# A gated-DeltaNet mixer written out in the order of its source, in a two-layer decoder trunk

## The chip, the core and the metric

The kernel runs on one core of a Trainium2 chip. A core has several engines, each with its own stream of instructions: TensorE (PE) for matrix products, VectorE (DVE), ScalarE (ACT), GpSimd (POOL) and SyncE (SP), which here mostly issues DMAs. They meet through semaphores. The metric is the device time of one execution in microseconds (us), the median of several.

## The reference

A trunk of two layers over 256 tokens of width 1024, in float32. Each layer is: half a SwiGLU FFN, a token mixer, cross-attention into 256 memory tokens, half a SwiGLU FFN, each behind an RMSNorm, with a residual sum. In layer 0 the mixer is dilated sliding-window attention beside a gated linear recurrence. In layer 1 it is the chunked gated DeltaNet:

```python
def deltanet_mixer(h, w_in, conv_w, a_log, dt_bias, o_norm, w_out):
    qkv, z, a, b = jnp.split(h @ w_in, [3 * W, 4 * W, 4 * W + DN_HEADS], axis=-1)
    qkv = jax.nn.silu(causal_dwconv(qkv, conv_w))          # 4 taps along the tokens
    q, k, v = jnp.split(qkv, 3, axis=-1)                   # 8 heads of 128
    q, k = l2norm(q.reshape(shp)), l2norm(k.reshape(shp))
    beta = jax.nn.sigmoid(b)
    g = -jnp.exp(a_log) * jax.nn.softplus(a + dt_bias)
    o = gated_delta_rule_chunked(q, k, v.reshape(shp), g, beta)  # chunks of 64: a triangular inverse,
    o = rmsnorm(o, o_norm) * jax.nn.silu(z.reshape(shp))         # then a state carried over the chunks
    return o.reshape(B, S, W) @ w_out
```

## The kernel before

Products are made to float32's accuracy from two parts: every weight and every moving operand is split into a high part and the rest. A weight arrives as `raw` by a DMA on SP; ScalarE copies it to its high part (L158), VectorE subtracts to get the low part (L159). One such conversion covers a half of a *unit*: 4 of the 8 blocks of 128 along the inner dimension, 256 columns wide. A unit is 256 columns of a weight against all tokens, in four *quarters*, each of 4 blocks for 128 columns (half of the unit's columns). In a quarter PE alternates a matmul of 512 columns (L200, high part) with one of 256 (L204, low part). After each quarter `tick` runs: after the first and the second it converts the two halves of the next unit's weight, and it runs pieces that fall due by the count of ticks (`self.after(n, fn)`).

The second mixer (in `mixer1`) has 16 units, in pairs of heads: `k0` is the keys of heads 0 and 1, likewise `q`, `v` and the gate `z`; `K2` and `K3` are units of the memory's keys and values for the cross-attention. `DN_ORDER` gives their order, with the groups of pairs `01` and `23` at the points where their recurrence is run:

```python
DN_ORDER = ('k0 k1 q0 q1 k2 v0 k3 v1 z0', '01|v3 z1 v2 q2', 'q3', '23|z2 z3 K2 K3')
```

Ahead of `k0` stand the normalisation (eight pieces: VectorE's product L409 into `xn`, ScalarE's high part L310, VectorE's rest L311 into `x2`) and a unit `ab` 128 columns wide for the gates a and b, with a softplus of 16 columns (L731 to L737). Each quarter-pair of a `k`, `q` or `v` unit is followed by `conv`: ScalarE copies the psum (L270), VectorE adds the second half of it (L271) into `xn`, ScalarE multiplies with the last tap (L1071), VectorE adds three more taps in place (L1074). When both halves are there, `silu` follows, as a tanh on ScalarE and a product on VectorE (L1080, L1081) for the units in `TWICE` (k0 k1 q0 q1), as ScalarE's own Silu (L1083) for the others. Then come squares (L1097) and sums over heads with a power of −1/2 on POOL (L341), the decays of a pair (`e`: a mask brought by SP, rows added by a DMA on POOL at L1119, exponentials at L1125, products at L1169), and a triangular inverse in steps (L1233 and L1235). The recurrence of a group (PE L1268 and L1274) runs in rounds; between rounds `fill(bg, n)` puts in n quarters of units from a background list. `DN_FILL` holds these numbers for the two groups. After it, `gated` (squares on ScalarE, POOL's power, VectorE L1332 and L1339) and `gated_T` (PE L1348, VectorE L1350 into `a`), and the output product.

The kernel is written in Tile, whose scheduler may move instructions within their engines: in before everything but the set-up has its order from it, and the source order counts only as a wish. In the first mixer, too, the heads' scores, weights and values are interleaved with quarters from a background list.

Of the kernel before, what the change touches and what calls it, by code (L numbers as in the profile page):

```python
# [9 lines left out]
F32 = mybir.dt.float32  # L10
# [3 lines left out]
AF = mybir.ActivationFunctionType  # L14
# [7 lines left out]
KD = 8  # L22
# [3 lines left out]
NEG = -1e30  # L26

DN_ORDER = ('k0 k1 q0 q1 k2 v0 k3 v1 z0', '01|v3 z1 v2 q2', 'q3', '23|z2 z3 K2 K3')
DN_FILL = ((1, 1, 1, 1, 1, 1, 1, 1, 1, 2, 2, 1), (1, 1, 1, 1, 1, 1, 1, 1, 1, 1, 1, 0, 5, 0))
YB = 5  # L30
EB, QB, VB = (4, 3, 3)
TWICE = 'k0 k1 q0 q1'.split()
# [35 lines left out]
class Net:  # L68
    def __init__(self, tc, t):
        self.tc, self.nc, self.t = tc, tc.nc, t  # L70
        self.raws, self.halves = {}, {}
        self.plan = list(self.make_plan())
        self.queue = [(i, k) for i, u in enumerate(self.plan) for k in range(0, u[4], 4)]

        self.queue[1], self.queue[2] = self.queue[2], self.queue[1]
        self.n_load = self.n_half = self.n_take = 0
        self.later = deque()
        self.banks, self.n_bank = "w", 0
        self.now, self.due = 0, []

# [62 lines left out]
    def split_half(self, step=4):  # L145

        nc = self.nc
        i, k = self.queue[self.n_half]
        name, l, _, _, nk, cols = self.plan[i]
        self.load_to(self.n_half + 1)  # L150
        n = min(4, nk - k)
        wt = self.p_wt.tile([P, 4, 2, 256], F32R, name="wt")
        raw = self.raws.pop(self.n_half)
        self.n_half += 1
        for u in range(0, n, step):
            us = slice(u, min(n, u + step))
            a, b, r = wt[:, us, 0, :cols], wt[:, us, 1, :cols], raw[:, us, :cols]
            nc.scalar.activation(a, r, AF.Copy)  # L158
            nc.vector.tensor_sub(b, r, a.bitcast(F32))  # L159
        self.halves.setdefault(i, []).append(wt)  # L160

    def w(self, name, c0):
# [10 lines left out]
    def tick(self):  # L173

        if self.n_half < len(self.queue) and self.queue[self.n_half][0] <= self.n_take:
            self.split_half()
        if self.later:
            self.later.popleft()()
        self.now += 1
        while self.due and self.due[0][0] <= self.now:  # L180
            self.due.pop(0)[2]()

    def after(self, n, fn):

# [5 lines left out]
    def mm3(self, out, wts, cols, mov, ks, k0=0, start=0, stop=KD):  # L190

        nc = self.nc
        for k in ks:
            i = k - k0
            w = wts[i // 4][:, i % 4]

            def high():
                nc.tensor.matmul(out.rearrange("p a s -> p (a s)"), w[:, 0, cols], mov[:, k].rearrange("p a s -> p (a s)"),  # L200
                                 start=k == start, stop=k == stop - 1)

            def low():
                nc.tensor.matmul(out[:, 0], w[:, 1, cols], mov[:, k, 0], start=False, stop=False)  # L204

            for part in (low, high) if k == stop - 1 else (high, low):
                part()

    def mm3t(self, out, mov, tok, wts, ks):

        nc = self.nc
        for k in ks:
            w = wts[k // 4][:, k % 4]

            def high():
                nc.tensor.matmul(out.rearrange("p a s -> p (a s)"), mov[:, k, 0, tok], w.rearrange("p a s -> p (a s)"),  # L216
                                 start=k == 0, stop=k == KD - 1)

            def low():
                nc.tensor.matmul(out[:, 0], mov[:, k, 1, tok], w[:, 0], start=False, stop=False)  # L220

            for part in (low, high) if k == KD - 1 else (high, low):
                part()
# [15 lines left out]
    def parts(self, out, a, b, first=True, last=True):  # L239

        for i, (u, w) in enumerate(((0, 0), (0, 1), (1, 0))):
            self.nc.tensor.matmul(out, a[u], b[w], start=first and i == 0, stop=last and i == 2)  # L242

    def unit_split(self, name, c0, mov, dst, tokens=False):

# [149 lines left out]
    def residual(self, k, ps, coef, gbase, parts=2):  # L395
        for i in range(parts):
            self.nc.vector.scalar_tensor_tensor(self.xT[:, k], ps[:, i], coef, self.xT[:, k],
                                                op0=OP.mult, op1=OP.add)
        if gbase == "sq":
            self.norm_sq(k)  # L400
        elif gbase is not None:
            self.norm_piece(k, gbase)
# [408 lines left out]
    def mixer0(self, mid, kT_mem, mem_mov, gnext):  # L811
        nc, tc, t = self.nc, self.tc, self.t
        mov = self.x2
        self.banks = "w"
        a2 = mid.tile([P, KD, 2, S], F32R, name="a2")
        with tc.tile_pool(name="m0", bufs=1, reuse_waits="tile") as mp:
# [9 lines left out]
            bg = deque()  # L826
# [33 lines left out]
            def scores(h):  # L860
                pr, par = divmod(h, 2)
                sc = self.bank("f")
                scf = sc.rearrange("p a b -> p (a b)")
                nc.tensor.matmul(scf[:, :P], qz[:, pr, par, :P], kT[:, pr, :P], start=True, stop=True)
                nc.tensor.matmul(scf[:, P:3 * P], qz[:, pr, par, P:], kT[:, pr], start=True, stop=True)
                pe = mp.tile([P, 2, S], F32, name="pe", bufs=3)
                mx = mp.tile([P, 2], F32, name="mx_a", bufs=3)
                nm = mp.tile([P, 2], F32, name="nm_a", bufs=3)
                den = mp.tile([P, 2], F32, name="den_a", bufs=3)
                rng = ((0, P), (P, 3 * P))  # L870
                for i, (u, w) in enumerate(rng):
                    nc.vector.tensor_tensor_reduce(pe[:, i, :w - u], scf[:, u:w], nmf[:, u:w], 1.0, NEG,
                                                   op0=OP.add, op1=OP.max, accum_out=mx[:, i:i + 1])
                nc.vector.tensor_scalar(nm, mx, -1.0, None, op0=OP.mult)
                for i, (u, w) in enumerate(rng):
                    nc.scalar.activation(pe[:, i, :w - u], pe[:, i, :w - u], AF.Exp, bias=nm[:, i:i + 1],
                                         accum_out=den[:, i:i + 1])
                return pe, den

            def weights(pe, den):  # L880
                ps = self.probs_T(pe, den, (P, 2 * P), mp)
                pT = mp.tile([P, 2, S], F32, name="pT_a", bufs=2)
                nc.scalar.activation(pT[:, 0], ps[:, 0], AF.Copy)
                nc.scalar.activation(pT[:, 1, P:], ps[:, 1, P:], AF.Copy)
                return pT

            def values(h, pT, po):

                pr, par = divmod(h, 2)
                o = po[:, par]  # L890
                vh = v[:, :, pr * P:pr * P + P]
                nc.tensor.matmul(o[:, :P], vh[:, 0], pT[:, 0, :P], start=True, stop=True)
                nc.tensor.matmul(o[:, P:], vh[:, 0], pT[:, 0, P:], start=True, stop=False)
                nc.tensor.matmul(o[:, P:], vh[:, 1], pT[:, 1, P:], start=False, stop=True)
                hs = slice(par * 64, par * 64 + 64)
                self.split(a2[hs, pr], o[hs])
# [52 lines left out]
            sc, pts, po = {}, {}, None  # L949
            for h in range(10):  # L950
                if h < 8:
                    sc[h] = scores(h)
                if 1 <= h < 9:
                    pts[h - 1] = weights(*sc.pop(h - 1))
                if h >= 2:
                    i = h - 2
                    if i % 2 == 0:
                        po = self.bank("s")
                    values(i, pts.pop(i), po)
                self.fill(bg, 2)  # L960
            self.fill(bg)
            self.flush()
            self.project_out("ab_w_out", a2, gnext)
# [37 lines left out]
    def mixer1(self, mid, kT_mem, mem_mov, gnext):  # L1001
        nc, tc, t = self.nc, self.tc, self.t
        mov = self.x2
        self.banks = "w"
        a2 = mid.tile([P, KD, 2, S], F32R, name="a2")
        with tc.tile_pool(name="m1", bufs=1, reuse_waits="tile") as mp:
            tok = lambda c: slice(c * P, c * P + P)

            nea, dtb = self.gate
# [376 lines left out]
            for i, part in enumerate(DN_ORDER):  # L1386
# [4 lines left out]
                group, bg = part.split("|")  # L1391
                gens = [back(int(p)) for p in group]
                bg = deque(unit(step) for step in bg.split())
                parts = list(DN_FILL[i // 2])
                if i == 1:
# [15 lines left out]
                    gated_T(int(p))  # L1411
                self.fill(bg)
            self.project_out("dn_w_out", a2, gnext)

    def finish(self):
        nc, tc = self.nc, self.tc
# [60 lines left out]
```

## Time and profile before

| | |
|---|---|
| median of 3 runs | 1252.77 us (1252.73 to 1253.04) |
| the profiled execution | 1251.99 us, of which the trace spans 1250.2 |
| PE busy | 1236.0 us, 99% |
| VectorE busy | 929.0 us, 74% |
| ScalarE busy | 752.0 us, 60% |
| conversions L159 / L158 | 484.9 us x409 / 418.6 us x409 |
| second mixer, first product to output product | 782.7 to 953.6 us |

An engine's busy time is the sum of its instructions' spans; a row of a timeline gives start, length, engine, line, operation, output and inputs, and in brackets how long the engine was idle before it and what it waited for. The line numbers are those of the kernel before.

### The profile page before, as it was taken

What the parts mean: (1) busy time and instruction counts of PE and PEld (TensorE: products, weight loads), DVE (VectorE), ACT (ScalarE), POOL (GpSimd) and SP (SyncE); (2) the same over time, 40 slices, a digit from 0 to 9 for tenths busy, and PEclk for the clock granted to TensorE, in tenths of its full rate; (3) what the DMA queues carried; (4) which work ended last, traced back from release to release, by engine and by line L of the source; (5) the groups of instructions that cost most, each with busy time, mean ns of one, the idle gap of its engine ahead of it and who ended that gap; (6) DMA issues with size and microseconds to landing.
All of it is one profiled execution on the core that took longest, in us unless ns stands there. A gap on an engine that the chain in (4) does not pass through costs nothing.

```text
span 1250.2 us, 20300 instructions
## 1 busy us (share of the span) xinstructions
PE 1236.0 (99%) x7702; PEld 1104.9 (88%) x7702; DVE 929.0 (74%) x1590; ACT 752.0 (60%) x1281; POOL 80.5 (6%) x96
## 2 busy tenths in 40 slices
PE   9999999999999999999999999999999999999997
PEld 8888889888998888888888888888898998888887
DVE  6987957788668778766877756989757668777753
ACT  7766545886555665545656544776757465666543
POOL 1000020000101000011000001020001101000000
PEclk9999999999999999999999999999999999999999
DMA  8766676544544566557666566667534535666561
GB/s 272 215 206 197 185 255 185 178 125 152 185 135 154 185 198 184 183 185 231 187 187 195 181 192 204 183 153 193 142 99 135 181 124 169 185 186 194 177 194 60
DMA packets 231019, 222.92 MB, mean 178 GB/s; under 512 B 14969, under 2 KB 228617, under 8 KB 230793
## 3 DMA queue, kind: packets, MB, share of 16 engines
q1 hardware_dynamic: 229448, 217.94, 56.9%
q0 software_dynamic: 1152, 3.15, 1.0%
q8 instruction: 60, 0.98, 0.3%
q10 hardware_dynamic: 320, 0.53, 0.1%
q14 instruction: 39, 0.31, 0.1%
HBM read 215.03 MB, written 5.51 MB: 176 GB/s over the span
## 4 chain that ended last, share of the span: by engine, by line
PE 90%; DVE 5%; ACT 2%; DMA 1%; issue 1%; POOL 1%; ACTq 0%; DVEq 0%; POOLq 0%
PE psw L200 21%; PE pss L200 16%; PE psw L204 11%; PE psf L200 11%; PE pss L204 8%; PE psf L204 5%; PE psw L242 5%; PE psf L242 4%; PE pss L242 3%; PE psw L216 2%; DVE wt L159 1%; PE psw L220 1%; ACT wt L158 1%; PE pss L1268 1%; PE psf L1274 1%
## 5 line engine op out<-in xcount | busy, mean ns | idle before, releaser
L159 DVE TENSOR_TENSOR wt<-raw,wt 128x1024 fp32r<-128x1024 f32 (+1 forms) x409 | 484.9, 1191 | 202.8 <-ACT wt L158 199.6
L158 ACT ACTIVATE wt<-raw 128x1024 fp32r<-128x1024 f32 (+1 forms) x409 | 418.6, 1031 | 172.1 <-PE psw L204 59.4
L200 PE MATMUL psw<-x,wt 128*128 128x512 f32 x864 | 310.6, 396 | 2.1 <-DVE xn L271 1.8
L204 PE MATMUL psw<-x,wt 128*128 128x256 f32 x864 | 224.9, 281 | 0.5 <-DVE wt L159 0.5
L200 PE MATMUL pss<-x,wt 128*128 128x512 f32 x520 | 187.4, 393 | 0.0
L200 PEld LDWEIGHTS psw<-x,wt 128*128 128x128 f32 x864 | 160.6, 188 | 30.1 <-issue 2.1
L204 PEld LDWEIGHTS psw<-x,wt 128*128 128x128 f32 x864 | 162.4, 188 | 9.4 <-DVE wt L159 1.0
L204 PE MATMUL pss<-x,wt 128*128 128x256 f32 x520 | 134.9, 280 | 0.0
L200 PE MATMUL psf<-x,wt 128*128 128x512 f32 x352 | 127.2, 394 | 0.0
L200 PEld LDWEIGHTS pss<-x,wt 128*128 128x128 f32 x520 | 97.7, 188 | 16.9 <-ACT bc L377 0.4
L204 PEld LDWEIGHTS pss<-x,wt 128*128 128x128 f32 x520 | 97.7, 188 | 5.4
L200 PE MATMUL psw<-h,wt 128*128 128x512 f32 x264 | 94.9, 396 | 0.0
L204 PE MATMUL psf<-x,wt 128*128 128x256 f32 x352 | 91.3, 280 | 0.0
L200 PE MATMUL pss<-h,wt 128*128 128x512 f32 x242 | 87.0, 396 | 0.0
L336 POOL TENSOR_TENSOR acc<-acc,sq 128x256 f32<-128x256 f32 x49 | 43.7, 891 | 658.3 <-ACT sq L334 557.3
L200 PEld LDWEIGHTS psf<-x,wt 128*128 128x128 f32 x352 | 66.1, 188 | 11.2
L204 PE MATMUL psw<-h,wt 128*128 128x256 f32 x264 | 72.0, 280 | 0.0
L204 PEld LDWEIGHTS psf<-x,wt 128*128 128x128 f32 x352 | 66.2, 188 | 3.5
L204 PE MATMUL pss<-h,wt 128*128 128x256 f32 x242 | 66.0, 280 | 0.0
L200 PEld LDWEIGHTS psw<-h,wt 128*128 128x128 f32 x264 | 49.6, 188 | 10.8
L200 PE MATMUL psf<-h,wt 128*128 128x512 f32 x154 | 55.4, 397 | 0.0
L200 PEld LDWEIGHTS pss<-h,wt 128*128 128x128 f32 x242 | 45.5, 188 | 9.8
(377 smaller groups left out, 2109.2 us busy)
## 6 DMA issues: line engine op xcount, KB each, us to landing
raw<-in_ffn_w_in_dram SPq DMA_DIRECT2D x175, 512.0 KB, 3.6
raw<-in_ffn_w_out_dram SPq DMA_DIRECT2D x80, 512.0 KB, 3.6
raw<-in_xa_wkv_dram SPq DMA_DIRECT2D x32, 512.0 KB, 3.5
raw<-in_dn_w_in_dram SPq DMA_DIRECT2D x32, 512.0 KB, 4.6
raw<-in_ab_w_in_dram SPq DMA_DIRECT2D x20, 512.0 KB, 3.6
raw<-in_xa_wq_dram SPq DMA_DIRECT2D x16, 512.0 KB, 3.5
raw<-in_xa_wo_dram SPq DMA_DIRECT2D x16, 512.0 KB, 3.4
raw<-in_ffn_w_out_dram SPq DMA_DIRECT2D x16, 256.0 KB, 2.9
```

Of the source, the lines that this page charges most:

```text
L158: nc.scalar.activation(a, r, AF.Copy)
L159: nc.vector.tensor_sub(b, r, a.bitcast(F32))
L200: nc.tensor.matmul(out.rearrange("p a s -> p (a s)"), w[:, 0, cols], mov[:, k].rearrange("p a s -> p (a s)"), start=k == start, stop=k == ...
L204: nc.tensor.matmul(out[:, 0], w[:, 1, cols], mov[:, k, 0], start=False, stop=False)
L216: nc.tensor.matmul(out.rearrange("p a s -> p (a s)"), mov[:, k, 0, tok], w.rearrange("p a s -> p (a s)"), start=k == 0, stop=k == KD - 1)
L220: nc.tensor.matmul(out[:, 0], mov[:, k, 1, tok], w[:, 0], start=False, stop=False)
L242: self.nc.tensor.matmul(out, a[u], b[w], start=first and i == 0, stop=last and i == 2)
L336: (eng or nc.gpsimd).tensor_add(self.acc, self.acc, sq)
L1268: nc.tensor.matmul(py[:, i], na[:, i], tu[:, 0, i], start=True, stop=True)
L1274: nc.tensor.matmul(pp[:, i], yy[:, i], tu[:, 1, i], start=True, stop=True)
```

## The change

It has three parts. First, the whole of `mixer1` is put under `tc.manual_schedule()`: there every engine's instructions stand in the order in which the source issues them, those of `tick` and the normalisation too. Second, the numbers of `DN_FILL` for the second group: one quarter less at two of its rounds and one less at the entry 5 (now 4), so that three stay for after the last rows of `gated_T`. Third, in the first mixer one of the two quarters after each head's step is moved to between its scores and its weights, and weights and values are pinned behind the last matmul issued so far (`issue_after`). The pin on due pieces in `tick` has no effect, since only `mixer1` uses them, where `pinned` is off.

```diff
-DN_FILL = ((1, 1, 1, 1, 1, 1, 1, 1, 1, 2, 2, 1), (1, 1, 1, 1, 1, 1, 1, 1, 1, 1, 1, 0, 5, 0))
+DN_FILL = ((1, 1, 1, 1, 1, 1, 1, 1, 1, 2, 2, 1), (1, 0, 1, 1, 0, 1, 1, 1, 1, 1, 1, 0, 4, 0))
...
         while self.due and self.due[0][0] <= self.now:
-            self.due.pop(0)[2]()
+            with self.behind():
+                self.due.pop(0)[2]()
+
+    def behind(self, engines=("pe", "act", "dve")):
+
+        stack = ExitStack()
+        for e in engines if self.pinned else ():
+            stack.enter_context(self.tc.issue_after(self.last[e].ins))
+        return stack
...
             for h in range(10):
                 if h < 8:
                     sc[h] = scores(h)
+                self.fill(bg, 1)
                 if 1 <= h < 9:
-                    pts[h - 1] = weights(*sc.pop(h - 1))
+                    with self.behind(("pe",)):
+                        pts[h - 1] = weights(*sc.pop(h - 1))
                 if h >= 2:
                     i = h - 2
                     if i % 2 == 0:
                         po = self.bank("s")
-                    values(i, pts.pop(i), po)
-                self.fill(bg, 2)
+                    with self.behind(("pe",)):
+                        values(i, pts.pop(i), po)
+                self.fill(bg, 1)
...
-        with tc.tile_pool(name="m1", bufs=1, reuse_waits="tile") as mp:
+        self.pinned = False
+        with tc.tile_pool(name="m1", bufs=1, reuse_waits="tile") as mp, tc.manual_schedule():
```

How this moves instructions, at three places. In the new kernel the shared helpers' lines are 9 higher (L271 is L280, L409 is L418, L311 is L320, L270 is L279) and those in `mixer1` 13 higher (L1071 is L1084, L1074 is L1087, L1083 is L1096, L1125 is L1138), L158 and L159 stay.

VectorE, in the first stretch of the second mixer, where k0's last half (`y_7953`) and k1's first (`y_8049`) are convolved; `dt` names belong to the softplus. Before:

```order
L271 TENSOR_TENSOR xn_8085<-psw_8054,xn_8085 128x256
L732 RECIPROCAL dtz_8013<-dtz_8013 128x16
L1074 SCALAR_TENSOR_TENSOR y_7953<-xn_8039,dcw_91,y_7953 128x253
L733 TENSOR_TENSOR dtz_8013<-dtz_8013,dte_8008 128x16
L159 TENSOR_TENSOR wt_8148<-raw_7956,wt_8148 128x4x256
L734 TENSOR_TENSOR dty_8014<-dtz_8013 128x16
L1081 SCALAR_TENSOR_TENSOR y_7953<-th_8046,y_7953 128x512
L735 TENSOR_SCALAR dts_8015<-dty_8014 128x16
L1074 SCALAR_TENSOR_TENSOR y_8049<-xn_8085,dcw_91,y_8049 128x255
```

Now, where q0 (`y_8136`) is convolved, with the two conversions beside it:

```order
L159 TENSOR_TENSOR wt_8150<-raw_7958,wt_8150 128x4x256
L280 TENSOR_TENSOR xn_8163<-psw_8141,xn_8163 128x256
L1087 SCALAR_TENSOR_TENSOR y_8136<-xn_8163,dcw_91,y_8136 128x255
L1087 SCALAR_TENSOR_TENSOR y_8136<-xn_8163,dcw_91,y_8136 128x254
L1087 SCALAR_TENSOR_TENSOR y_8136<-xn_8163,dcw_91,y_8136 128x253
L159 TENSOR_TENSOR wt_8170<-raw_8052,wt_8170 128x4x256
L1119 TENSOR_SCALAR ss_8189<-pss_8184 128x4
L1157 RECIPROCAL r2_8193<-ss_8189 128x4
L1158 TENSOR_TENSOR nb_all_7944<-nbeta_7937,r2_8193 128x2x2
L280 TENSOR_TENSOR xn_8212<-psw_8174,xn_8212 128x256
L1087 SCALAR_TENSOR_TENSOR y_8136<-xn_8212,dcw_91,y_8136 128x255
```

Conversions, sums and the three taps of a half now follow each other, with the small operations between them at one place; before, the taps of one half stood between conversions and sums of another.

VectorE, at the normalisation ahead of the second mixer (`xn` the product, `x2` the rest, `wt` of 128 columns the weight of the unit `ab`). Before:

```order
L409 SCALAR_TENSOR_TENSOR xn_7824<-xT_78,prm_90,bc_7822 128x256
L409 SCALAR_TENSOR_TENSOR xn_7828<-xT_78,prm_90,bc_7822 128x256
L159 TENSOR_TENSOR wt_7882<-raw_7764,wt_7882 128x4x128
L311 TENSOR_TENSOR x2_79<-xn_7824,x2_79 128x256
L311 TENSOR_TENSOR x2_79<-xn_7828,x2_79 128x256
L409 SCALAR_TENSOR_TENSOR xn_7832<-xT_78,prm_90,bc_7822 128x256
L409 SCALAR_TENSOR_TENSOR xn_7836<-xT_78,prm_90,bc_7822 128x256
```

Now, the last pieces of the eight:

```order
L418 SCALAR_TENSOR_TENSOR xn_7850<-xT_78,prm_90,bc_7824 128x256
L320 TENSOR_TENSOR x2_79<-xn_7850,x2_79 128x256
L418 SCALAR_TENSOR_TENSOR xn_7854<-xT_78,prm_90,bc_7824 128x256
L320 TENSOR_TENSOR x2_79<-xn_7854,x2_79 128x256
L159 TENSOR_TENSOR wt_7871<-raw_7713,wt_7871 128x4x128
L280 TENSOR_TENSOR kT_7759<-psw_7862,kT_7759 128x256
L159 TENSOR_TENSOR wt_7884<-raw_7766,wt_7884 128x4x128
```

Product and rest of each piece now alternate, and both conversions for `ab` stand behind the eighth piece; before, pieces went in twos with the conversions among them.

ScalarE, in the first stretch, where the function changes between Silu and Exp (ACT_TABLE_LOAD brings the table of the function that follows). Before:

```order
L1071 ACTIVATE y_8306<-xn_8387,dcw_91 128x256
L1125 ACTIVATE e_7952<-e_7952,ngc_7939 128x128 x2
L270 ACTIVATE xn_8443<-psw_8405 128x256
L1125 ACTIVATE e_7952<-e_7952,ngc_7939 128x128 x2
L158 ACTIVATE wt_8517<-raw_8309 128x4x256
L1071 ACTIVATE y_8400<-xn_8443,dcw_91 128x256
L1083 ACT_TABLE_LOAD
L1083 ACTIVATE y_8306<-y_8306 128x512
```

Now:

```order
L1096 ACT_TABLE_LOAD
L1096 ACTIVATE y_8308<-y_8308 128x512
L158 ACTIVATE wt_8416<-raw_8228 128x4x256
L1110 ACTIVATE th_8419<-y_8308 128x512
L279 ACTIVATE xn_8445<-psw_8407 128x256
L1084 ACTIVATE y_8402<-xn_8445,dcw_91 128x256
L158 ACTIVATE wt_8452<-raw_8309 128x4x256
L1138 ACT_TABLE_LOAD
L1138 ACTIVATE e_7953<-e_7953,ngc_7941 128x128 x4
L1138 ACTIVATE e_7954<-e_7954,ngc_7941 128x128 x4
```

The Silu of k2 now comes before the exponentials of pairs 2 and 3, and a third table load follows at v0's Silu; before, one load stood behind all exponentials.

More of the change, by code (lines that the diff above doesn't have):

```diff
@@ L78, in __init__ @@
         self.banks, self.n_bank = "w", 0
-        self.now, self.due = 0, []
+        self.now, self.due, self.last, self.pinned = 0, [], {}, True
     def make_plan(self):
@@ L157, in split_half @@
             a, b, r = wt[:, us, 0, :cols], wt[:, us, 1, :cols], raw[:, us, :cols]
-            nc.scalar.activation(a, r, AF.Copy)
-            nc.vector.tensor_sub(b, r, a.bitcast(F32))
+            self.last["act"] = nc.scalar.activation(a, r, AF.Copy)
+            self.last["dve"] = nc.vector.tensor_sub(b, r, a.bitcast(F32))
         self.halves.setdefault(i, []).append(wt)
@@ L199, in high @@
             def high():
-                nc.tensor.matmul(out.rearrange("p a s -> p (a s)"), w[:, 0, cols], mov[:, k].rearrange("p a s -> p (a s)"),
-                                 start=k == start, stop=k == stop - 1)
+                self.last["pe"] = nc.tensor.matmul(out.rearrange("p a s -> p (a s)"), w[:, 0, cols],
+                                                   mov[:, k].rearrange("p a s -> p (a s)"),
+                                                   start=k == start, stop=k == stop - 1)
             def low():
@@ L215, in high @@
             def high():
-                nc.tensor.matmul(out.rearrange("p a s -> p (a s)"), mov[:, k, 0, tok], w.rearrange("p a s -> p (a s)"),
-                                 start=k == 0, stop=k == KD - 1)
+                self.last["pe"] = nc.tensor.matmul(out.rearrange("p a s -> p (a s)"), mov[:, k, 0, tok],
+                                                   w.rearrange("p a s -> p (a s)"), start=k == 0, stop=k == KD - 1)
             def low():
@@ L241, in parts @@
         for i, (u, w) in enumerate(((0, 0), (0, 1), (1, 0))):
-            self.nc.tensor.matmul(out, a[u], b[w], start=first and i == 0, stop=last and i == 2)
+            self.last["pe"] = self.nc.tensor.matmul(out, a[u], b[w], start=first and i == 0, stop=last and i == 2)
     def unit_split(self, name, c0, mov, dst, tokens=False):
@@ L1413, in mixer1 @@
             self.project_out("dn_w_out", a2, gnext)
+        self.pinned = True
     def finish(self):
```

## The prediction

> **What bounds the kernel.** I read first the page's head and busy times, then the stretches of the second mixer, then the groups of its first stretch kept apart by form.
>
> ```profile
> span 1250.2 us, 20300 instructions
> PE 1236.0 (99%) x7702; PEld 1104.9 (88%) x7702; DVE 929.0 (74%) x1590; ACT 752.0 (60%) x1281; POOL 80.5 (6%) x96
> ```
> ```profile
> core 0: us, PE busy (x) PEld busy (x) DVE busy (x) ACT busy (x) POOL busy (x), PEclk, DMA share, GB/s
> 787.40:850.30 62.90, 60.38 (x380) 53.22 (x379) 56.68 (x168) 49.06 (x104) 9.35 (x9) 1.00 0.67 169
> 850.30:902.60 52.30, 51.20 (x357) 46.39 (x356) 41.87 (x108) 35.68 (x86) 3.27 (x3) 1.00 0.66 178
> 902.60:953.60 51.00, 49.66 (x362) 45.96 (x361) 31.12 (x64) 34.96 (x82) 4.20 (x4) 1.00 0.27 85
> ```
>
> TensorE bounds the whole, 99%. But in the first stretch (from the conversion for k1 to the one at z0's first tick, eight units, 62.9/8 = 7.86 us each) VectorE is at 90% and ScalarE at 78%. They carry that load only because they overlap: 56.68 + 49.06 = 105.7 us of work in 62.9 us. Two engines that wait for each other in turn do not fit in there.
>
> ```profile
> L159 DVE TENSOR_TENSOR wt<-raw,wt 128x1024 fp32r<-128x1024 f32 x17 | 20.7, 1218 | 0.6 <-ACT wt L158 0.5
> L158 ACT ACTIVATE wt<-raw 128x1024 fp32r<-128x1024 f32 x18 | 19.0, 1059 | 4.4 <-PE psw L204 3.7 <-PE psw L200 0.7
> L1071 ACT ACTIVATE y<-xn,dcw 128x256 f32<-128x256 f32 x15 | 7.5, 503 | 1.7 <-DVE xn L271 1.6
> L1074 DVE SCALAR_TENSOR_TENSOR y<-xn,dcw,y 128x255 f32<-128x255 f32 x15 | 7.1, 476 | 1.1 <-ACT y L1071 1.1
> L1074 DVE SCALAR_TENSOR_TENSOR y<-xn,dcw,y 128x254 f32<-128x254 f32 x15 | 7.1, 474 | 0.0
> L1074 DVE SCALAR_TENSOR_TENSOR y<-xn,dcw,y 128x253 f32<-128x253 f32 x15 | 7.0, 469 | 0.0
> L271 DVE TENSOR_TENSOR xn<-psw,xn 128x256 f32<-128x256 f32 x17 | 7.0, 413 | 0.1
> L341 POOL TENSOR_TENSOR rs_dn<-ss,mhalf 128x4 f32<-128x4 f32 x5 | 7.0, 1396 | 55.2 <-DVE ss L1106 49.4 <-DVE ti L1235 5.8
> ...
> L1125 ACT ACTIVATE e<-e,ngc 128x128 f32<-128x128 f32 x16 | 5.4, 390 | 4.0 <-DMA e<-gd 4.0
> ...
> L1169 DVE SCALAR_TENSOR_TENSOR na<-psf,nb_all,e 128x128 f32<-128x128 f32 x12 | 3.8, 342 | 1.5 <-ACT e L1125 1.5
> ...
> L1080 ACT ACTIVATE th<-y 128x512 f32<-128x512 f32 x4 | 2.5, 622 | 0.0
> ...
> L737 DVE SCALAR_TENSOR_TENSOR dts<-dts,dty 128x16 f32<-128x16 f32 x7 | 1.2, 169 | 0.0
> ...
> L1233 DVE TENSOR_TENSOR tm<-nb,ti 64x63 f32<-64x63 f32 x2 | 0.4, 209 | 0.0
> ```
>
> The column after the bar is busy time and mean ns; the last shows almost no waiting for ScalarE (1.1 us over 45 taps of L1074, 0.5 over 17 conversions). VectorE's timeline shows why: between the steps of one half's convolution it does other work.
>
> ```profile
> 812.23 0.45 DVE L1074 SCALAR_TENSOR_TENSOR y<-xn,dcw,y 128x255 f32<-128x255 f32 x1
> 812.60 0.42 DVE L271 TENSOR_TENSOR xn<-psw,xn 128x256 f32<-128x256 f32 x1
> ...
> 813.40 1.22 DVE L159 TENSOR_TENSOR wt<-raw,wt 128x1024 fp32r<-128x1024 f32 x1
> 814.53 0.87 DVE L1074 SCALAR_TENSOR_TENSOR y<-xn,dcw,y 128x253 f32<-128x253 f32 x2
> ```
>
> **Conversions and convolutions in source order.** Nothing is removed from these; they only change places. In the new order VectorE has, per unit, one conversion, one half's sum L271, its three taps, the second conversion, the second sum, its taps; ScalarE has copy, multiply L1071, copy, multiply, then the unit's L1080. Each sum feeds a multiply on the other engine, which feeds the taps; the conversion stands behind taps, not in the gap. Round one unit: L158 1.06, L159 1.22, L271 0.41, L1071 0.50, three taps 0.48 + 0.47 + 0.47 = 1.42, L159 1.22, L271 0.41, L1071 0.50, taps 1.42, L1080 0.62, sum 8.78. (The second copy lies beside the first taps, L1081 beside the next copy.) The six changes of engine cost what this pair shows:
>
> ```profile
> 821.03 0.49 ACT L1071 ACTIVATE y<-xn,dcw 128x256 f32<-128x256 f32 x1
> 821.55 0.48 DVE L1074 SCALAR_TENSOR_TENSOR y<-xn,dcw,y 128x255 f32<-128x255 f32 x1 [0.30 <-ACT y L1071]
> ```
>
> that is 0.03 each, 0.2, less as much where neighbours on one engine overlap: 8.9 us a unit against 7.86. PE needs the second conversion for its next unit, so it waits. Over eight units 71.2 − 62.9 = +8.3.
>
> **Small operations in the same row.** In before they fall into gaps; now they lengthen the round. k0, softplus: 17 dependent small operations of 0.17 (as L737) = 2.9, and an exponential and a transpose awaited, about 0.8 each, 4.5. k1, decays: 1.9. q0, q1: three operations of that size each, 1.0 together. k2: four L1169, 1.4, a table load 1.3, sums and a wait for POOL, 0.7: 3.4. v0: two table loads, 2.6, and eight L1125 at 0.39, each overlapping the next a little, 2.5: 5.1. k3: thirty steps of the inverse (L1233, L1235) at 0.20, 6.0. v1: 1.1. Together 23.0. With the 8.3: **+31.3**.
>
> Two of these table loads are new (Silu at k2, Exp again for the decays of pairs 2 and 3, Silu at v0; before has one here). Its price:
>
> ```profile
> 830.14 0.50 ACT L1071 ACTIVATE y<-xn,dcw 128x256 f32<-128x256 f32 x1
> 830.65 1.28 ACT L1083 ACT_TABLE_LOAD   x1
> 831.95 0.63 ACT L1083 ACTIVATE y<-y 128x512 f32<-128x512 f32 x1
> ```
>
> From the end of L1071 to the start of L1083 it is 1.31 us. The Trainium skill ("ScalarE: Activation LUTs", section "What ACT_TABLE_LOAD costs") adds a drain of about 1.38 us to the 1283 ns of the load, for 2.66 us a switch, which would make the two new ones cost 2.7 us more than I count. Here the trace differs: nothing stands between the neighbours but 0.03 us, so the sum keeps 1.31.
>
> The mask transfers on SP and the loads L1119 on POOL stand in source order too, a place or two from where they stood among raw's loads and L341. In before the exponentials L1125 waited 4.0 us for them, 1.5 of it passed on to L1169 and on to PE's 1.84 at 820.62 (its row is below). I cost them at nothing, since the exponentials themselves come some 15 us later; without that cover it is those 4.0 again.
>
> **The entry.** Before, the normalised pieces are made two at a time and PE begins the stage's first product on early ones:
>
> ```profile
> 777.77 0.88 DVE L409 SCALAR_TENSOR_TENSOR xn<-xT,prm,bc 128x256 f32<-128x256 f32 x2 [0.24 <-ACT bc L377]
> 778.29 0.81 ACT L310 ACTIVATE x<-xn 128x256 fp32r<-128x256 f32 x2
> 779.17 0.76 DVE L311 TENSOR_TENSOR x<-xn,x 128x256 fp32r<-128x256 f32 x2
> ...
> 782.71 0.40 PE L200 MATMUL psw<-x,wt 128*128 128x512 f32 x1
> ...
> 785.77 0.39 PE L200 MATMUL psw<-x,wt 128*128 128x512 f32 x1
> ```
>
> Now each L311 follows its own L409 and waits for L310: 0.44 + 0.41 + 0.38 = 1.23 a piece, eight pieces 9.8, so 787.6. Behind them stands the 512-column conversion for that product, some 0.7 and a hand-over: start 788.3 to 789, against 782.71, then k0 3.06 later as now. I take **+6.0** (ends 4.8, if neighbours overlap everywhere, and 7.1, if k0's conversion also comes late). PE idles about 5 us in one piece here.
>
> **The two group stages.** From 850.30 to 902.60 four units with convolutions cost 4 x 1.0 = 4.1. VectorE is held at the gated rows by POOL, as here:
>
> ```profile
> 899.90 0.17 DVE L1332 TENSOR_TENSOR ro_all<-ro,rq_all 128x4 f32<-128x4 f32 x1 [0.90 <-POOL ro L341]
> ```
>
> but twice for the 1.40 of L341 and its neighbours, 1.6 each = 3.2, with nothing let past; ScalarE's squares add 2.2. **+9.5**. After 902.60 VectorE is at 61% of the stretch, so only chains count: the copy awaited by PE for the state 3.3, the rows after it 2.7, the last gated rows 2.9, less about 3.0 of waits that are there now: **+5.9**. These two are walked by hand and less certain: from 0, if PE's own work hides them, to twice.
>
> **The kept quarters and the first mixer.** Two quarters are taken from rounds of the second group and one from its last entries, so that three stand behind the last gated rows: this takes away a wait that is shown below, already in the 5.9. Pinning the first mixer's heads and moving one of two fills ahead removes 0.70 at 292.00 and may delay a softmax: **−0.5** (−1.2 to +1.5).
>
> ```profile
> 820.62 0.47 PE L200 MATMUL psw<-x,wt 128*128 128x512 f32 x1 [1.84 <-DVE xn L271]
> 953.60 0.50 PE L200 MATMUL psf<-a,wt 128*128 128x512 f32 x1 [1.34 <-DVE a L1350]
> 292.00 0.30 PE L658 MATMUL pss<-ident,pe 128*128 128x128 f32 x1 [0.70 <-DVE pe L656]
> ```
>
> **Sum.** 6.0 + 31.3 + 9.5 + 5.9 − 0.5 = +52.2. The profiled execution took 1251.99 (span 1250.2); the median of the runs is 1252.77, 0.8 above it. 1252.0 + 52.2 + 0.8 = 1305.
>
> **Rivals.**
> - *Only the first stretch costs.* PE's own 51.2 and 49.7 us of work after 850.3 and 902.6 cover the group stages, where VectorE has 20% and 39% free: 6.0 + 31.3 = +37, 1290 (1283 to 1293 with half of the small operations hidden). Against: the chains alternate, so free time is no cover. 14%.
> - *PE slows after each long wait.* The chain shows the same four matmuls at twice the time near the start, after PE had been idle:
>
> ```profile
> 4.62 0.93 PE psf L429 x4
> 6.83 0.62 PE pss L429 x4
> 12.69 0.44 PE psf L429 x4
> ```
>
> Half rate until about 6.8 loses some 1.1 us; full rate is seen by 12.7, so at most about 2. Some ten waits of 3 us or more (entry, k0, k2, v0, k3, the groups' ends) would add 11 to 20: 1316 to 1325. Against: the granted clock is 1.00 in all three stretches, and none of its waits is that long, so they don't say. 17%. The Trainium skill ("TensorE: Matmul & The Clock Gate", section "What's actually happening") has PE at half rate after one idle window of about 3.4 us and until a busy one; by that rule each such wait would cost about 1.7 us, an estimate from the page, which is this rival's middle.
> - *Not slower.* If a unit's round closes within 7.86 us, PE sets the pace as now. That needs the chain of 8.78 to lose 0.9, which happens if the engines run a copy ahead of the sum (L158 of the next half while PE still works, 1.06 out of the round) and the small operations wait on nothing. Then the order takes away 1.84 + 1.34 + 0.70 and about 1 elsewhere: 1247 to 1253. The three taps depend on one another and on L1071 in any order, which speaks against it. 6%.
>
> **How the numbers follow.** The forecast, 1293 to 1316 by the bounds of its terms, has 63%, the two slower rivals 14 and 17, the last 6. The likeliest is 1305. The range of 8 in 10 takes in the upper part of the first rival and most of the second: 1284 to 1322. A measurement of this kernel tells 0.2% (2.5 us) from no change. Slower 94%; of the last rival's 6, faster 4 and same 2.
>
> **What would show it.** Right: between the conversions for k1 and at z0 some 94 us instead of 62.9; L1074 and L159 with long idle times put down to L1071 and L158; PE waiting for L159 at nearly every unit; three table loads on L1083 and L1125 in the stage; k0 about 6 later than the first piece; PE not waiting at 953.60's place. The clock rival: a granted clock under 1.00 in the first stretch, and runs of like matmuls at twice their time, as at 4.62. Wrong: PE busy over 95% of that stretch, with VectorE's idle time small. Largest risk to the size: the small operations' 23.0, if many lie beside ScalarE's copies.

## The result and the profile after

The changed kernel takes 1322.35 us (median of 5, 1320.1 to 1324.92) against 1252.77: a ratio of 1.0548, 95% interval 1.0531 to 1.0564, or +69.6 us. Forecast were 1305 (+52.2) and a range of 1284 to 1322, so the direction held and the time lies 0.4 us past the upper end. It also lies past 1293 to 1316, the bounds of the forecast's own terms, and inside the 1316 to 1325 of the rival that PE slows after long waits. The profiled execution spans 1318.7 us, 68.5 more than before. From its page: span, busy times, and the chain of waits by engine.

```profile
span 1318.7 us, 20296 instructions
PE 1259.8 (96%) x7702; PEld 1118.2 (85%) x7702; DVE 940.0 (71%) x1590; ACT 756.7 (57%) x1283; POOL 77.4 (6%) x96
...
PE 79%; DVE 10%; ACT 7%; issue 2%; DMA 2%; SPq 0%; POOL 0%; ACTq 0%; DVEq 0%; POOLq 0%
```

Before, the chain had PE at 90%, VectorE at 5%, ScalarE at 2%: PE lost 11 points, and VectorE and ScalarE gained five each. By stages, each ended by the same instruction in both traces (the last but one ends here at the output product's first matmul, 949.23 before; the prediction had set its end 4.4 us later, at that product's wait at 953.60; to there, 1016.52 now, it is +11.7, and +5.6 behind it):

| stage | before | after | difference | forecast |
|---|---|---|---|---|
| to the conversion for k1 (forecast: entry 6.0, first mixer −0.5) | 787.40 | 795.01 | +7.6 | +5.5 |
| to z0's first tick (first stretch) | 62.93 | 94.77 | +31.8 | +31.3 |
| to the second group's first L1268 | 52.26 | 64.07 | +11.8 | +9.5 |
| to the output product | 46.64 | 59.86 | +13.2 | +5.9 |
| to the end | 300.97 | 304.99 | +4.0 | 0 |

The same view of stretches as before, of the changed kernel (length, busy time of PE, PEld, VectorE, ScalarE and POOL, granted clock, DMA share):

```profile
795.00:889.80 94.80, 72.18 (x374) 59.95 (x372) 66.47 (x172) 50.47 (x101) 8.70 (x9) 0.86 0.46 121
889.80:953.80 64.00, 53.63 (x363) 47.80 (x363) 41.07 (x100) 35.36 (x86) 3.02 (x3) 1.00 0.50 133
953.80:1013.70 59.90, 53.84 (x345) 48.04 (x345) 31.05 (x62) 35.06 (x83) 4.03 (x4) 0.92 0.25 79
```

In the first stretch VectorE fell from 90% to 70% and ScalarE from 78% to 53%: no engine is full. The groups of that stretch say who waits for whom:

```profile
L208 PE MATMUL psw<-x,wt 128*128 128x512 f32 x124 | 50.9, 448 | 4.7 <-ACT wt L158 4.6
L213 PE MATMUL psw<-x,wt 128*128 128x256 f32 x124 | 35.7, 310 | 7.3 <-DVE wt L159 7.3
...
L159 DVE TENSOR_TENSOR wt<-raw,wt 128x1024 fp32r<-128x1024 f32 x17 | 20.8, 1222 | 8.1 <-ACT wt L158 8.1
...
L1084 ACT ACTIVATE y<-xn,dcw 128x256 f32<-128x256 f32 x16 | 8.1, 509 | 27.1 <-DVE xn L280 27.1
L1087 DVE SCALAR_TENSOR_TENSOR y<-xn,dcw,y 128x255 f32<-128x255 f32 x16 | 7.7, 484 | 9.2 <-ACT y L1084 9.2
...
L280 DVE TENSOR_TENSOR xn<-psw,xn 128x256 f32<-128x256 f32 x16 | 6.7, 416 | 4.0 <-ACT xn L279 4.0
```

The durations are those of before (1222 against 1218 ns, 484 against 476). What grew is the last column: ScalarE's multiply waits 27.1 us for VectorE's sum (1.6 before), the taps 9.2 for the multiply (1.1), the conversions 8.1 for ScalarE's copy (0.5), and PE 11.9 for the two parts of a conversion. One unit (q0), VectorE's timeline:

```profile
823.79 1.22 DVE L159 TENSOR_TENSOR wt<-raw,wt 128x1024 fp32r<-128x1024 f32 x1
...
825.40 0.42 DVE L280 TENSOR_TENSOR xn<-psw,xn 128x256 f32<-128x256 f32 x1
826.40 1.52 DVE L1087 SCALAR_TENSOR_TENSOR y<-xn,dcw,y 128x255 f32<-128x255 f32 x3 [0.58 <-ACT y L1084]
...
828.95 0.69 DVE L1094 SCALAR_TENSOR_TENSOR y<-th,y 128x512 f32<-128x512 f32 x1 [0.96 <-ACT th L1093]
829.90 1.23 DVE L159 TENSOR_TENSOR wt<-raw,wt 128x1024 fp32r<-128x1024 f32 x1 [0.26 <-ACT wt L158]
```

ScalarE's, and PE's two waits, in the same time:

```profile
825.85 0.51 ACT L1084 ACTIVATE y<-xn,dcw 128x256 f32<-128x256 f32 x1 [1.50 <-DVE xn L280]
828.29 0.63 ACT L1093 ACTIVATE th<-y 128x512 f32<-128x512 f32 x1 [1.92 <-DVE hb_all L1159]
828.82 1.05 ACT L158 ACTIVATE wt<-raw 128x1024 fp32r<-128x1024 f32 x1
```
```profile
825.06 0.39 PE L213 MATMUL psw<-x,wt 128*128 128x256 f32 x1 [1.25 <-DVE wt L159]
831.18 0.38 PE L213 MATMUL psw<-x,wt 128*128 128x256 f32 x1 [0.76 <-DVE wt L159]
```

ScalarE waits 1.50, works 0.51, and VectorE waits 0.58 for that; ScalarE waits 1.92 for the taps (the profile names L1159, the small operation right behind them on VectorE), and VectorE 0.96 for L1093. The copy L158, which depends on nothing there, stands behind L1093, so the next conversion is late and PE waits.

The entry: the first and the last L320, the conversion behind them, and PE.

```profile
778.58 0.43 DVE L320 TENSOR_TENSOR x<-xn,x 128x256 fp32r<-128x256 f32 x1 [0.48 <-ACT x L319]
...
787.71 0.43 DVE L320 TENSOR_TENSOR x<-xn,x 128x256 fp32r<-128x256 f32 x1 [0.48 <-ACT x L319]
788.23 0.69 DVE L159 TENSOR_TENSOR wt<-raw,wt 128x512 fp32r<-128x512 f32 x1
```
```profile
788.25 0.80 PE L208 MATMUL psw<-x,wt 128*128 128x512 f32 x1 [5.53 <-ACT wt L158]
788.97 0.58 PE L213 MATMUL psw<-x,wt 128*128 128x256 f32 x1
789.35 0.63 PE L208 MATMUL psw<-x,wt 128*128 128x512 f32 x1
...
789.99 0.63 PE L208 MATMUL psw<-x,wt 128*128 128x512 f32 x1
```

Seven pieces from 778.58 to 787.71 are 1.30 each (1.23 forecast). PE waits 5.53, and the matmuls behind it run at about half rate: one of 512 and one of 256 columns together take 0.64 (789.35 to 789.99) instead of the 0.35 before (782.71 to 783.06).

### The profile page after: what moved, and what is told of

Same layout as the page of the kernel before. It is cut to its first block, busy times and chain, and to the rows that moved or that the text cites. A ratio compares the mean times of both kernels' runs of the same rounds, so it can differ in the third digit from the quotient of the medians.

```text
span 1318.7 us, 20296 instructions
## 1 busy us (share of the span) xinstructions
PE 1259.8 (96%) x7702; PEld 1118.2 (85%) x7702; DVE 940.0 (71%) x1590; ACT 756.7 (57%) x1283; POOL 77.4 (6%) x96
## 4 chain that ended last, share of the span: by engine, by line
PE 79%; DVE 10%; ACT 7%; issue 2%; DMA 2%; SPq 0%; POOL 0%; ACTq 0%; DVEq 0%; POOLq 0%
PE psw L208 18%; PE pss L208 14%; PE psf L208 10%; PE psw L213 9%; PE pss L213 7%; PE psf L213 5%; PE psw L251 4%; PE psf L251 4%; DVE wt L159 3%; PE pss L251 2%; ACT wt L158 2%; DVE y L1087 2%; PE psw L225 1%; ACT y L1084 1%; PE psf L1287 1%
## 5 line engine op out<-in xcount | busy, mean ns | idle before, releaser
L159 DVE TENSOR_TENSOR wt<-raw,wt 128x1024 fp32r<-128x1024 f32 (+1 forms) x409 | 484.8, 1190 | 222.1 <-ACT wt L158 219.3
L158 ACT ACTIVATE wt<-raw 128x1024 fp32r<-128x1024 f32 (+1 forms) x409 | 417.9, 1029 | 162.0 <-PE psw L213 54.5
L208 PE MATMUL psw<-x,wt 128*128 128x512 f32 x864 | 320.6, 406 | 10.5 <-ACT wt L158 10.1
L213 PE MATMUL psw<-x,wt 128*128 128x256 f32 x864 | 229.0, 285 | 8.2 <-DVE wt L159 8.2
L208 PEld LDWEIGHTS psw<-x,wt 128*128 128x128 f32 x864 | 164.9, 193 | 40.0 <-ACT wt L158 12.2
L213 PEld LDWEIGHTS psw<-x,wt 128*128 128x128 f32 x864 | 166.4, 193 | 20.9 <-DVE wt L159 12.3
L208 PEld LDWEIGHTS psw<-h,wt 128*128 128x128 f32 x264 | 49.6, 188 | 10.8
```

The source lines that it names most:

```text
L158: self.last["act"] = nc.scalar.activation(a, r, AF.Copy)
L159: self.last["dve"] = nc.vector.tensor_sub(b, r, a.bitcast(F32))
L208: self.last["pe"] = nc.tensor.matmul(out.rearrange("p a s -> p (a s)"), w[:, 0, cols], mov[:, k].rearrange("p a s -> p (a s)"), start=k == ...
```

## The experiments

Times are medians; the runs of the kernel before, beside these, lay between 1250.9 and 1258.7, which the ratios take in. Theory: two engines in order take turns where the schedule had overlapped them, and PE waits for what is late by that. Rivals: PE's half rate carries much of the loss; the other parts of the change do; or the groups cost nothing.

### Which part of the change it is

`order_only`: the new order, the old `DN_FILL` and the old first mixer.

```diff
-DN_FILL = (..., (1, 0, 1, 1, 0, 1, 1, 1, 1, 1, 1, 0, 4, 0))
+DN_FILL = (..., (1, 1, 1, 1, 1, 1, 1, 1, 1, 1, 1, 0, 5, 0))
```

> Only the source order in the second mixer; DN_FILL's numbers and the first mixer's heads are those of the kernel before. Theory (the order costs it all): about 1322, within 3 us of the changed kernel's 1322.4. Rival (the three kept quarters or the pinned heads cost or save several us): 1315 or less, or 1330 or more.

1318.17, ratio 1.0516 (1.0494 to 1.0539). The order alone costs nearly all. The kept quarters save nothing under it: the traces have 1314.5 with the old numbers and 1318.7 with the new ones, though the two intervals meet, so the 4 us are not certain. In the traces they lie behind the first group (times in us):

| stage | before | `rest_only` | `order_only` | changed |
|---|---|---|---|---|
| second group, to the output product | 46.64 | 48.47 | 54.15 | 59.86 |
| from the output product to the end | 300.97 | 299.01 | 307.09 | 304.99 |

So the kept quarters move about 2 us from the end into the second group in either order, and in source order the second group grows by 3.7 more. It holds as many matmuls with the old numbers as with the new ones; they keep PE busy for 49.77 us at a granted clock of 0.97, and for 53.84 at 0.92 in the changed kernel (its row is above).

```profile
953.20:1007.40 54.20, 49.77 (x346) 45.42 (x345) 26.95 (x57) 32.33 (x76) 4.03 (x4) 0.97 0.24 78
```

`rest_only`: everything but the order.

```diff
-        with tc.tile_pool(name="m1", bufs=1, reuse_waits="tile") as mp, tc.manual_schedule():
+        with tc.tile_pool(name="m1", bufs=1, reuse_waits="tile") as mp:
```

> The kept quarters and the pinned heads without the source order: the second mixer is scheduled as in the kernel before. Theory: 1251 to 1254, that is within 0.2% of the 1252.8 before (the prediction gave these parts -0.5, -1.2 to +1.5). Rival: they interact, and 1257 or more is theirs.

1254.82 against 1252.99 of the runs beside it, ratio 1.0004 (0.9991 to 1.0018): no difference. Its profile also shows a likely part of why such runs spread by 4 us, a wait of ScalarE for the memory's load at the start of the program. It was 0.9 us in the profile before, 1.9 in the changed kernel's and 4.1 here:

```profile
ACT m L571 <- DMA mem<-in_mem_dram: 4.1, 1, 4.1
```

### Which stage it is

`first_only` and `groups_only` switch the source order off, or on, where the first group's recurrence begins.

```diff
             for i, part in enumerate(DN_ORDER):
+                if i == 1:
+                    man.close()      # groups_only: man.enter_context(tc.manual_schedule())
```

> Source order only from the entry to the end of the first stretch (up to z0), the groups and all behind them scheduled. Theory: 7.6 + 31.8 = 39.4 us, 1285 to 1296. Rival (the scheduled groups take part of it back): under 1280.

> Source order only from the first group's recurrence on; entry and first stretch are scheduled as in the kernel before. Theory (each stage pays for itself): 11.8 + 13.2 + 4.6 = 29.6 us, the differences of the two group stages and the end between the two traces, so 1276 to 1288. Rival (the groups pay only because the first stretch leaves them late, the prediction's rival with 14%): under 1262.

1292.75, ratio 1.0312 (1.0284 to 1.0340), and 1285.24, ratio 1.0252 (1.0224 to 1.0279), beside 1255.0: +37.8 and +30.2, together 68.0 against the 69.6 of the whole. So the stages pay each for itself. With the entry and the first stretch late by 41 us (94.8 us in that stretch), the scheduled groups take 52.8 and 48.5 us, against 52.3 and 46.6 before and 52.2 and 48.5 in `rest_only`, which has the same kept quarters. With an early first stretch the groups in source order take 64.2 and 61.2. The rival that PE's work covers the groups is out.

The scheduled first stretch of `groups_only` is itself 3.3 longer than before. Every engine has the same instructions there in the same order. But behind one wait of 2.01 us (1.84 before, at 820.62) PE ran at a granted clock of 0.56 up to 825 and of 0.76 up to 830, and the same 380 matmuls kept it busy for 63.57 us instead of 60.41:

```profile
786.80:853.05 66.25, 63.57 (x380) 56.18 (x379) 56.79 (x169) 49.28 (x104) 9.14 (x9) 0.95 0.63 160
```
```profile
820.16 0.47 PE L208 MATMUL psw<-x,wt 128*128 128x512 f32 x1 [2.01 <-DVE xn L280]
```

So where PE has no other waits, slow matmuls behind one wait cost their full price, here 3.2 us.

### Whether PE's half rate carries it

`warm`: spare matmuls in PE's two longest waits.

```diff
             pab = self.bank_w()
+            keep(pab, 22)            # 22 matmuls of 512 columns, overwritten later
...
                 pgc = self.bank("s")
+                keep(pgc, 18)
```

> The changed kernel with spare matmuls (their results are overwritten) where PE waits longest: 22 of 512 columns ahead of the first product (wait of 5.7 us), 18 ahead of the decays' sums (wait of 5.0 us). Theory A (ScalarE's and VectorE's chain sets the pace, the slow matmuls lie beside it): no shorter than 1320. Theory B (the half-rate matmuls after the waits are on the path): 2.3 + 2.0 = 4.3 us shorter, about 1318. In both the matmuls behind these two waits run at full rate.

```profile
782.65 5.16 PE L1029 MATMUL psw<-m 128*128 128x512 f32 x22
788.33 0.51 PE L208 MATMUL psw<-x,wt 128*128 128x512 f32 x1 [0.53 <-ACT wt L158]
...
789.28 0.40 PE L208 MATMUL psw<-x,wt 128*128 128x512 f32 x1
```

The matmuls behind the wait run at full rate (0.40 at 789.28), and from the first product to the conversion for k1 it takes 5.0 us instead of 6.8. From there to z0's first tick it takes 94.75 us, as without the spare matmuls (94.77), so the slow ones behind the second wait lay beside the chain of the two other engines. But the total is 1321.09, ratio 1.0540 (1.0517 to 1.0564), not told apart from 1.0548: the first group took 66.25 us instead of 64.07. The same 363 matmuls kept PE busy there for 55.58 us at a granted clock of 0.96, against 53.70 at 1.00, so half rate came back in another place:

```profile
888.10:954.35 66.25, 55.58 (x363) 49.34 (x364) 41.15 (x100) 35.53 (x86) 3.02 (x3) 0.96 0.47 129
```

The number is theory A's; but with the slow matmuls moved and not taken away, the run doesn't say what they cost in the groups. For that the second group has a hint. Five kernels run it with the same instructions in the same order on every engine, and its length follows PE's busy time there (us):

| | `entry` | changed | `k2_tanh` | `groups_only` | `warm` |
|---|---|---|---|---|---|
| length | 58.56 | 59.86 | 60.12 | 61.19 | 61.49 |
| PE busy | 53.72 | 53.80 | 54.22 | 54.88 | 56.19 |
| granted clock | 0.93 | 0.92 | 0.91 | 0.90 | 0.88 |

Before, PE's work took 46.64 us there. So the order alone doesn't fix that stage's length, and slow matmuls are likely a part of it; how large a part is not shown.

### Whether the turn-taking is the cause

`entry`: the source order begins behind the normalisation.

```diff
             self.covered([self.mem_key(c, mem_mov, kT_mem) for c in range(2)], mp, C_MIX + 8)
+            man.enter_context(tc.manual_schedule())
```

> The changed kernel with the source order beginning only behind the normalisation, which is scheduled as before. Theory: the first product comes back from 788.3 to about 782.7, PE's 5.7 us wait and the half-rate matmuls behind it are gone, the total 5.5 to 7.6 us shorter, about 1316. Rival (the first stretch's turn-taking has slack that takes the gain in): 1320 or more.

1315.39, ratio 1.0480 (1.0446 to 1.0515): 7.0 shorter. The first product starts at 782.38, the conversion for k1 at 788.10, 6.9 earlier. The first stretch kept its length (94.62). In the trace the first group took 3.7 of the gain back (67.76, with PE at a granted clock of 0.94) and the second gave 1.3, so that the two profiled executions differ by 4.6 only.

`pipe`: still source order, but the source is written so that the engines overlap. (`LATE` is 2. What follows Silu has its offset cut by `LATE`, so that all but the keys' squares keeps its place.)

```diff
             def conv(y, j, f, ps):
                 x = mp.tile([P, S], F32, name="xn", bufs=2)
+                half = self.half_copy() if self.by_conv and self.can_half(1) else None   # ScalarE
                 self.add(x, ps)
                 nc.scalar.activation(y[:, j], x, AF.Copy, scale=tap(3))
+                if half:
+                    self.half_sub(half)                                                  # VectorE
                 for i in (2, 1, 0):
...
-                silu(y, twice)
+                self.after(LATE, rest)     # silu and all that follows it
```

> The changed kernel, still in source order on every engine, but with the source written so that the engines overlap: ScalarE's copy of the next half-unit stands ahead of a half's sum, VectorE's part of that conversion between the sum and the taps, and Silu with all that follows two quarters later. Theory A (it is the turn-taking of the two engines): a unit's round falls from 8.9 to about 7 us, the first stretch from 94.8 to 70 to 80, the total to 1298 to 1308. Rival (small operations and their waits in the row): the stretch stays over 88, the total over 1314. Rival (manual order costs something by itself): no change.

1311.44, ratio 1.0467 (1.0446 to 1.0488), 10.9 shorter; the first stretch 88.6. The stretch missed the theory's 70 to 80 and lies with its rival's, the total lies between the two. That source order costs something by itself, whatever the order, is out. PE now waited in its own row four times, 19.9 us in all, for a Silu or its tanh form that comes later; the longest:

```profile
856.04 0.69 PE L1196 MATMUL psf<-ident,y 128*128 128x128 f32 x2 [7.65 <-ACT y L1126]
```

`pipe_rows` puts those transposes four quarters later, `pipe_all` adds `entry` and moves the decays' sums two quarters later and their rows one.

```diff
-KST = (0, 7 - LATE, 3 - LATE)
+KST = (0, 7 - LATE, 7 - LATE)
...
-AB = (3, 5, 8, 10, 11, 12, 12)
+AB = (3, 7, 9, 10, 11, 12, 12)   # pipe_all only
```

> As pipe (conversions between sums and taps, Silu two quarters later), and the keys' transposes on PE stand four quarters later, since in pipe PE waited for Silu at them four times, 20.5 us in all. Theory (turn-taking; those waits hide nothing else): the first stretch falls from 88.6 to 70 to 76, the total to 1293 to 1299. Rival (VectorE's and ScalarE's small operations are the bound anyway): it stays over 84, the total over 1306.

> As pipe_rows, and the normalisation scheduled as before, and the decays' sums on PE two quarters later (wait of 4.3 in pipe). Theory: 5.5 from the entry and 4 to 6 from the decays less than pipe_rows, 1281 to 1289; what is left over the kernel before is then in the two group stages (about +20). Rival: new waits take the place of those, 1295 or more.

1308.39 (ratio 1.0425, 1.0387 to 1.0463) and 1301.78 (1.0375, 1.0348 to 1.0401), first stretch 84.9 and 83.1. Both missed the theory's numbers. `pipe_rows` lies with its rival, that the small operations are the bound, and `pipe_all` with its own, that new waits take the place of the old. Which of the two it is, ScalarE's and VectorE's timelines of `pipe_rows` show:

```profile
813.69 0.63 ACT L1140 ACTIVATE th<-y 128x512 f32<-128x512 f32 x1 [2.13 <-DVE y L1124]
814.22 1.04 ACT L158 ACTIVATE wt<-raw 128x1024 fp32r<-128x1024 f32 x1
```
```profile
815.57 0.42 DVE L307 TENSOR_TENSOR xn<-psw,xn 128x256 f32<-128x256 f32 x1 [1.92 <-ACT xn L306]
```

The square waits 2.13 for VectorE's product; the copy and the next unit's L306 stand behind it, and VectorE waits 1.92 for that. It is the same turn-taking one step further on. `pipe_squares` is `pipe_all` with the squares two quarters later.

```diff
-KST = (0, 7 - LATE, 7 - LATE)
+KST = (2, 7 - LATE, 7 - LATE)
-QST = (2 - LATE, 9 - LATE, 5 - LATE)
+QST = (4 - LATE, 9 - LATE, 5 - LATE)
```

> As pipe_all, and the squares L1140 on ScalarE stand two quarters later: in pipe_rows ScalarE waited there 2.2 us for VectorE's L1124 four times, with the next unit's copy and sum behind it. Theory (turn-taking, wherever two neighbours depend on each other): the first stretch falls by 6 to 9 us from 83.1, the total from 1301.8 to 1292 to 1297. Rival (what is left is VectorE's own work, 63.2 us busy there): 1300 or more.

1296.28, ratio 1.0341 (1.0317 to 1.0365): as expected, 5.5 shorter, the first stretch 76.7. So the 83.1 were new waits and not bounded by the small operations. Its view of that stretch, and the group that still waits most:

```profile
788.10:864.80 76.70, 64.10 (x363) 55.01 (x362) 62.82 (x168) 47.51 (x95) 8.70 (x9) 0.93 0.56 145
```
```profile
L1113 ACT ACTIVATE y<-xn,dcw 128x256 f32<-128x256 f32 x15 | 7.6, 510 | 20.2 <-DVE xn L307 20.2
```

So from the changed kernel's 94.8 the stretch comes to 76.7 by changes in the source's order alone, all of it in source order. Of the 31.8 us lost there 18.1 are shown to be order; some work was put off into the first group, which grew from 64.1 to 68.9, so net it is 13.3. The other 13.7 are not settled one by one; ScalarE's 20.2 us of waiting for VectorE points the same way.

### Two single prices

`k2_tanh`: k2's Silu as tanh and product; two table loads fall away.

```diff
-TWICE = 'k0 k1 q0 q1'.split()
+TWICE = 'k0 k1 q0 q1 k2'.split()
```

> The changed kernel with k2's Silu made by a tanh on ScalarE and a product on VectorE, as the first four units have it; by that two of the table loads of the first stretch fall away. By the trace's price (1.31 a load) and VectorE's extra product (0.69): the first stretch shrinks by 1.9 to 2.6 us from 94.8, the total by about 2. By 2.66 a switch (the Trainium skill, ScalarE: Activation LUTs): by 4.6 to 5.3. Rival (ScalarE's loads lie beside VectorE's work): no shorter.

The first stretch goes from 94.77 to 92.10, by 2.7 us: 1.25 in k2's unit and 1.43 in v0's, where the two loads stood. The total is 1319.99 (ratio 1.0517, 1.0482 to 1.0552), not told apart. That is the trace's price of 1.31 a load, not the 2.66 of the Trainium skill ("ScalarE: Activation LUTs", section "What ACT_TABLE_LOAD costs"). The changed kernel's rows have no drain either (1.28, and 0.02 to the Silu):

```profile
862.78 1.28 ACT L1096 ACT_TABLE_LOAD   x1 [1.63 <-DVE tm L1246]
864.08 0.63 ACT L1096 ACTIVATE y<-y 128x512 f32<-128x512 f32 x1
```

`rows_later`: the first group's `gated_T` five quarters later, for PE's longest wait in the groups:

```profile
952.89 1.17 PE L1361 MATMUL pss<-ident,qk 128*128 128x128 f32 x4 [4.03 <-DVE qk L1352]
```
```diff
-                        self.after(4 + n, lambda p=int(p): gated_T(p))
+                        self.after(9 + n, lambda p=int(p): gated_T(p))
```

> The changed kernel with the first group's gated_T five quarters later, where PE waited 4.2 us for VectorE's L1352, which waited for POOL. Theory: that wait is hidden, 3 to 4.2 us shorter, about 1318. Rival (the next wait in the row takes its place): no shorter than 1321.

1325.7 (ratio 1.0575, 1.0537 to 1.0612): no shorter, the rival's. (The profiled execution begins the first product 5.7 us late, with 4.2 of the wait for the memory's load.) The wait at 952.89 is gone and the first group takes 59.04 us instead of 64.07, but the second takes 66.32 instead of 59.86; from the first product to the output product it is 227.6 us instead of 225.5. In the second group's first rounds PE now waits 3.44 and 1.33.

No version beat the kernel before; `rest_only` equals it.

## Why the prediction was right, and where it was short

- **The unit's round and the small operations** (+31.3): +31.8, and not by luck. From one unit's first conversion to the next it takes (forecast: a round of 8.9 and the unit's small operations):

| | k0 | k1 | q0 | q1 | k2 | v0 | k3 | v1 |
|---|---|---|---|---|---|---|---|---|
| forecast | 13.4 | 10.8 | 9.4 | 9.4 | 12.3 | 14.0 | 14.9 | 10.0 |
| measured | 14.62 | 10.58 | 9.69 | 9.42 | 12.26 | 14.10 | 14.13 | 9.96 |

  The steps are those of the timeline above: conversions, sums and taps follow in turn, and PE waits for L159 or L158. The 1.2 more in k0 are the size of a table load for the softplus (L758, 1.28 at 800.77), which the forecast left out. The masks and rows, put at nothing, cost nothing here: L1138 waits for no transfer.
- **The entry** (+6.0): the first product came 5.5 late, and the half-rate matmuls behind its wait made it 7.6 at the conversion for k1. `entry` took 6.9 of it back there. The term was short by those matmuls, which the prediction had kept for a rival; `warm` gives them 1.7.
- **The first group** (+9.5): +11.8. PE's idle time there grew by 9.3, from 1.10 to 10.37. VectorE's waits for POOL's power, L1345 below, are there twice as forecast, 1.12 each; but they were there before too (0.90 each), and new are 1.33 each for ScalarE's squares. PE also waits 1.3 for the transfer of the inverse (`tu`), which it did not before.

```profile
951.08 0.17 DVE L1345 TENSOR_TENSOR ro_all<-ro,rq_all 128x4 f32<-128x4 f32 x1 [1.12 <-POOL ro L350]
```

- **The second group** (+5.9) **and the output product** (nothing) are the step that failed: +13.2 and +4.0, or +7.5 and +6.1 without the kept quarters (`order_only`). The output product is inside the new order and was counted as a gain only, at the wait of 1.34; its units wait for conversions as the others do, and so +6.1 was put at nothing. That price is the same with the kept quarters in both (304.99 against 299.01 in `rest_only`, 6.0). And of the 3.0 taken off for "waits that are there now" only that 1.34 was there: from 902.59 to 949.23 PE lost nothing before. PE's idle time in the second group, 6.1, is near the forecast; the other 7.2 are matmuls that kept it busy for 53.8 us instead of 46.6, which no term had. Whether faster ones would have made the stage shorter or only the waits longer stays open. The first row here is of the second group, the other two of the output product:

```profile
961.28 1.05 PE L1116 MATMUL pss<-ones,th 128*128 128x1 f32 x8 [2.73 <-DVE a L1363]
...
1027.59 0.49 PE L208 MATMUL psw<-a,wt 128*128 128x512 f32 x1 [1.04 <-ACT wt L158]
1028.85 0.39 PE L213 MATMUL psw<-a,wt 128*128 128x256 f32 x1 [0.76 <-DVE wt L159]
```

- **The kept quarters and the first mixer** (−0.5): without the order nothing (ratio 1.0004), with it rather a loss of about 4 by the traces of `order_only`, nearly all of it in the second group (5.7 longer, 2.1 of it back behind it). As forecast, PE has no wait at the output product's start any more.
- **The rivals.** That only the first stretch costs is out by `groups_only`, +30.2. PE's half rate is there, with both signs the prediction named: a granted clock of 0.86 and 0.92, and like matmuls at nearly twice their time. The total lies in this rival's 1316 to 1325. It explains 1.7 us at the entry and nothing that shows in the first stretch, where `warm` took one such place away and the units came out as forecast without it. In the second group it may explain several us and is not ruled out; `groups_only` shows 3.2 us for one place where PE is the bound. That POOL's and SP's moves cost nothing was not tested alone.

## What to carry to other kernels

Where two engines that run their instructions in order are each over three quarters busy and hand work to one another, the order on each decides whether their times overlap or add: look in the timeline for an instruction without dependencies (here the copy L158) that stands behind one which waits. Before fixing such an order by hand, add up one round along its hand-overs, as instructions and not as shares of busy time, and do so for every part that the new order takes in, the last product too. Taking away one wait in such a row brought less than the wait nearly every time (`pipe_rows` 3.7 us of the stage for waits of 19.9, `rows_later` nothing for 4.03), so the row is to be judged by the length of its stage.

## What the runs showed of the hardware

PE fell to half rate behind shorter waits than the entry's 5.53 us: behind 2.01 us in `groups_only` (820.16, above), behind 2.63 us at 850.66, and behind 0.91 us at 1008.31, where it had done only eight short transposes and one matmul since 1004.24. Behind the 1.84 us at 820.62 before it did not.

```profile
850.66 0.55 PE L1166 MATMUL psf<-ident,y 128*128 128x128 f32 x2 [2.63 <-ACT y L1096]
...
851.65 0.63 PE L208 MATMUL psw<-x,wt 128*128 128x512 f32 x1
```
```profile
1005.09 2.07 PE L1361 MATMUL pss<-ident,qk 128*128 128x128 f32 x8 [0.85 <-DVE qk L1352]
...
1008.31 0.58 PE L213 MATMUL psw<-m,wt 128*128 128x256 f32 x1 [0.91 <-DVE wt L159]
1008.69 0.63 PE L208 MATMUL psw<-m,wt 128*128 128x512 f32 x1
```

Full rate came back about 4.3 us after the entry's wait ended (788.25 to 792.6). The Trainium skill ("TensorE: Matmul & The Clock Gate", section "What's actually happening") asks for an idle window of about 3.4 us; these unbroken waits were shorter, 2.63 us at most, which suggests that the share of work in a stretch of time counts rather than an unbroken pause. What share it is, these runs don't show.
